# Merge gates take the place of retention's first head in the gaps of the projections, and the branch projections start inside the attention stage

## The chip, the cores and the metric

The kernel runs on one core of one Trainium2 chip, in one launch. The metric is device microseconds (us) of that core, the median of several runs; less is better. Engines are named as the profile names them: PE is TensorE (PEld its weight loads), DVE VectorE, ACT ScalarE, POOL GpSimd, SP the engine that issues most DMAs.

## The reference

One decoder block on x (1024 tokens by 1024 channels, float32). Only the parts around the change are spelt out.

```python
h = rms_norm(x, norm1_g)
z = h @ w_in                         # zq, zkv, zg (attention), zr (retention), zm (merge gates)
y_nsa = nsa_attention(zq, zkv, zg)   # compressed + selected + sliding-window branches, 8 heads of 64
y_ret = retention(q, k, v, g)        # zr: 4 parts (q, k, v, g) x 4 heads x 128 columns
u = einsum('nbsc,ncd->bsnd', stack([y_nsa, y_ret]), w_branch)     # two 512 -> 1024 projections
gates = sigmoid(zm)                  # 2 x 1024 columns of z
x = x + sum(gates * u) @ w_out
x = x + (silu(h2 @ w_gate) * (h2 @ w_up)) @ w_down                # h2 = rms_norm(x, norm2_g)
```

## The kernel before

**Order of the work.** The kernel writes a static program for each engine. A small planner inside the kernel decides the order while the program is built: every piece of work is a generator ("stream") that yields one instruction at a time; the planner keeps a modelled free time for each engine, and always emits the instruction that could start first by its model (ties on PE go to the lower priority number). On the chip each engine then runs its own list in order. So a stream with a high number fills PE wherever the streams of attention are, by the model, not ready; in this document such work is called fill.

**Matmuls.** All large products are float32 operands split in two parts (high and low), three matmuls of 128x128 by 128x512 for each block. A weight column tile of 128 columns over 1024 channels and 1024 tokens takes 2 halves x 8 x 3 = 48 matmuls (`half_mm`, 24 for each half). Where two such tiles are done together by the Winograd form of Strassen's scheme, the pair takes seven products of 12 matmuls, 84 in place of 96 (`g_main`, `g_prod`); its operand sums are made by DVE from the halves of H (`g_sums`), and of the weights (`g_wsums`, `g_fill`).

**Stages, in order of time.** (1) Norm, transposes and the token-major projections for q, k, v and the compressed branch (`a_mm`). In the gaps of the last of these, `ret_plain` runs the four projections of retention's head 0 plainly: k, v, q and g, 4 x 48 matmuls; what doesn't fit in the gaps follows them. (2) `g_main`: heads 1 to 3 of retention as six pairs of seven products each. (3) Attention (`cmp_all`, `produce_all`, `consume_all`), 16 units (2 groups x 8 query blocks), with retention's recurrence (`retention`) beside it, and as fill `merge_gates`: 16 column tiles, whose tanh ACT writes to tile zs and SP stores to z_scr. (4) When the last gate is done, the tile H (the normed input, no longer needed) is written over by the split outputs of the two branches (`y_loads`, `y_split`: tiles yraw to H); `branch1` multiplies retention's output with its half of w_branch, 16 half tiles of 12 matmuls in the two PSUM banks of f_ring, and `branch1_out` multiplies each by its gate (tile sg, loaded from z_scr) and stores it in u_scr. Stage 4 needs retention's pool to be closed (`late`). (5) `merge_main` waits for branch1 and for the last attention unit, and does the same 16 half tiles for the attention branch in the six banks of u_ring; `merge_out` loads gate and u_scr (tiles sgm and mx) and adds. (6) Output projection (`out_main`), norm, and the feed-forward part, which the change doesn't touch.

DMAs of these streams are all issued by SP, in the planner's order, but for the q tiles and group loads of attention, which POOL issues. DVE and ACT each run one list for all streams. `us` lists the attention units; `("y", us[-1])` is set when the last has been stored.

Of the kernel before, what the change touches and what calls it, by code (L numbers as in the profile page):

```python
# [9 lines left out]
F32 = mybir.dt.float32  # L10
F32R = mybir.dt.float32r
I32 = mybir.dt.int32
AF = mybir.ActivationFunctionType
# [3 lines left out]
T = 1024  # L17
# [241 lines left out]
def kernel(  # L259
# [199 lines left out]
    m_units = [[ntile(win, M0 + b * D + c * 128) for b in range(2)] for c in range(8)]  # L459
    rings = {"wo": None}  # L460
    o_units = [Unit(w_out[0][k * 128:(k + 1) * 128, :], lambda: rings["wo"]) for k in range(8)]
    r_plain = r_units[0]
    r_pairs = [(h, i) for h in range(1, 4) for i in (2, 0)]
    order = [u for c in range(7, -1, -1) for u in m_units[c][::-1]] + b_units[1] + b_units[0] + o_units

    def half_mm(hl, half, o, k0=0, nk=8, mov=None, step=1):
        n = 0
# [331 lines left out]

    def weights():  # L800
        yield Wait(lambda: "cmp" in fl)
        yield from split_units(r_plain)

    sch.spawn(load_units(r_plain), 5)
    sch.spawn(weights(), 3)
    sch.run(lambda: "cmp" in fl)
    cp.close()
# [21 lines left out]
    def unit(u):  # L829
        yield Wait(lambda: u.hl is not None)  # L830
# [9 lines left out]
        gm["S", j] = gpr.tile([128, 2, 4, 512], F32R, name=f"gS{j}")  # L840
    gt_ring = Bag([gpr.tile([128, 512], F32, name=f"gt{n}") for n in range(3)])

    def ret_plain():
        yield Wait(lambda: "rt" in fl)
        for i, u in enumerate(r_plain):
            yield from unit(u)
            for half in range(2):
                o = yield Alloc(f_ring)
                yield from half_mm(u.hl, half, o)
                t = yield Alloc(gt_ring)  # L850
                if i == 3:
                    yield ac(t, o, func=AF.Tanh, scale=0.5)
                    yield stt(t, t, 1.0, o, ALU.add, ALU.mult)
                else:
                    yield ac(t, o)
                f_ring.release(o)
                yield dma(r_scr[0][i][:, half * 512:half * 512 + 512], t)
                gt_ring.release(t)
            u.release()
        fl.add("plain")  # L860
# [55 lines left out]
    graw_ring = Slots([g_raw(n) for n in range(4)], lambda n: n % 4)  # L916

    def g_loads():
        yield Wait(lambda: all(u.raw is not None for u in r_plain))
        gm["raw"] = [(yield Alloc(raw_ring)), (yield Alloc(raw_ring))]  # L920
        for f, (h, i) in enumerate(r_pairs):
            if f:
                yield Wait(lambda: "gp" in fl)
            for n in range(2):
                t = yield Alloc(graw_ring)
                yield dma(t, r_units[h][i + n].src)
                gm["GU"[n], f] = t
        fl.add("gl")
        for i in range(2):
            yield Wait(lambda: i not in graw_ring.held)  # L930
            raw_ring.release(gm["raw"][i])
        yield from load_units(order)
# [7 lines left out]
    gop_ring = Slots([g_op(n) for n in range(8)], lambda n: n % 8 if n < 7 * GN - 6 else 4 + n % 4)  # L940

    def g_ops():
        yield Wait(lambda: all(u.hl is not None for u in r_plain))
        gm["h"] = [(yield Alloc(hl_ring))]
        made = set()
        for n, (p, f) in enumerate(gseq):
            yield Wait(lambda: ("G", f) in gm)
            G = gm["G", f]
            if n == 2:
                gm["h"].append((yield Alloc(hl_ring)))  # L950
            if n >= 4:
                yield Wait(lambda: "gp" in fl)
            if p in (1, 2):
                src, then = G[:, 4 * p - 4:4 * p], None
            else:
                yield Wait(lambda: ("U", f) in gm)
                U = gm["U", f]
                if p in (5, 6) and f not in made:
                    made.add(f)
                    sch.spawn(g_wsums(f, G, U), 2)  # L960
                if p == 5:
                    yield Wait(lambda: f in gT1)
                    src, then = gT1[f], lambda f=f: g_drop(f)
                elif p == 6:
                    yield Wait(lambda: f in gT2)
                    src, then = gT2[f], lambda f=f: fl.add(("g6", f))
                elif p == 7:
                    yield Wait(lambda: f in gT2)
                    src = yield Alloc(gm["Ta"])
                    yield tt(src, U[:, 4:8], U[:, 0:4], ALU.subtract)  # L970
                    then = lambda c=src: gm["Ta"].release(c)
                elif p == 4:
                    yield Wait(lambda: f in gT4)
                    src, then = gT4[f], lambda f=f: gm["Tb"].release(gT4[f])
                else:
                    src, then = U[:, 4:8], lambda U=U: graw_ring.release(U)
            o = yield Alloc(gop_ring)
            sch.spawn(g_fill(p, f, o, src, then), 2)
        for i in range(2):
            yield Wait(lambda: all(2 * i + j not in gop_ring.held for j in range(2)))  # L980
            hl_ring.release(gm["h"][i])
        yield from split_units(order)
# [215 lines left out]
        fl.add("ret")  # L1198

    sch.spawn(g_sums(), 7, 500.0)  # L1200
    sch.spawn(ret_plain(), 6)
    sch.spawn(g_loads(), 5)
    sch.spawn(g_ops(), 3)
    sch.spawn(g_main(), 8)
# [54 lines left out]
    zp_ring = ps_ring("S")  # L1259

    def merge_gates():
        for c in range(7, -1, -1):
            for b in (1, 0):
                um = m_units[c][b]
                yield from unit(um)
                z_scr[c, b] = dram.tile([128, T], F32, name=f"z_scr{c}_{b}")
                for half in range(2):
                    ring = f_ring if ("ret" in fl or "r0" not in fl) and f_ring.can() else zp_ring
                    o = yield Alloc(ring)
                    yield from half_mm(um.hl, half, o)  # L1270
                    sch.spawn(gate_out(c, b, half, o, ring), 4)
                um.release()
        fl.add("gates")
# [296 lines left out]
        fl.add(("u1", c, half))  # L1570

    def merge_main():
        yield Wait(lambda: "b1" in fl and ("y", us[-1]) in fl)
        for c, half in b0_order:
            yield from unit(b_units[0][c // 2])
            sch.spawn(merge_out(c, half), 1)
            yield from branch_mm(0, c, half, u_ring)
            if c % 2 and half:
                b_units[0][c // 2].release()
        fl.add("u_done")  # L1580

    b0_order = [(c, half) for c in range(4) for half in range(2)] + [(c, half) for half in range(2) for c in range(4, 8)]

    def mx_loads():
        for c, half in b0_order:
# [1 line left out]
            yield dma(mx[c // 2][:, c % 2, s], u_scr[c][:, s])  # L1587
            fl.add(("mx", c, half))

    def merge_out(c, half):  # L1590
        s = slice(half * 512, half * 512 + 512)
        yield Wait(lambda: ("mx", c, half) in fl)
        m = mx[c // 2][:, c % 2, s]
        sgm = yield Alloc(sg_ring)
        yield dma(sgm, z_scr[c, 0][:, s])
        yield Wait(lambda: (c, 0, half) in ups)
        yield stt(sgm, sgm, 1.0, ups[c, 0, half], ALU.add, ALU.mult)
        u_ring.release(ups[c, 0, half])
        yield tt(m, m, sgm, ALU.add)
        fl.add(("mix", c, half))  # L1600
        sg_ring.release(sgm)
# [6 lines left out]
    lts = ExitStack()  # L1608
    lt = lts.enter_context(tc.tile_pool(name="lt", bufs=1, side="right"))
    late["yraw"] = sb_ring(lt, [128, 512], F32, "yraw", 6)  # L1610
    late["sg"] = sb_ring(lt, [128, 512], F32, "sg", 4)
    fl.add("late")
    sch.run(lambda: ("y", us[-1]) in fl)
    sch.run(lambda: all(("yt", b, half, k) in fl for b in range(2) for half in range(2) for k in range(4))
# [699 lines left out]
```

## Time and profile before

| | us |
|---|---|
| median of 3 runs (lowest, highest) | 1615.13 (1609.12, 1615.92) |
| the profiled execution | 1612.77 |
| its span, first to last instruction | 1611.0 |
| PE busy in the span | 1564.9 (97%) |
| DVE busy | 1084.1 (67%) |
| ACT busy | 737.4 (46%) |
| mean granted PE clock | 0.992 of full |

Busy time is the union of an engine's instructions. The profile's rows give, for a group of instructions, how many there are, their busy time, the mean of one, and the idle time of the engine just before them with what ended it. A granted clock of 1.00 is 2.4 GHz, 0.5 is 1.2 GHz, and a stretch with a value between saw both.

### The profile page before, as it was taken

What the parts mean: (1) busy time and instruction counts of PE and PEld (TensorE: products, weight loads), DVE (VectorE), ACT (ScalarE), POOL (GpSimd) and SP (SyncE); (2) the same over time, 40 slices, a digit from 0 to 9 for tenths busy, and PEclk for the clock granted to TensorE, in tenths of its full rate; (3) what the DMA queues carried; (4) which work ended last, traced back from release to release, by engine and by line L of the source; (5) the groups of instructions that cost most, each with busy time, mean ns of one, the idle gap of its engine ahead of it and who ended that gap; (6) DMA issues with size and microseconds to landing.
All of it is one profiled execution on the core that took longest, in us unless ns stands there. A gap on an engine that the chain in (4) does not pass through costs nothing.

```text
span 1611.0 us, 23610 instructions
## 1 busy us (share of the span) xinstructions
PE 1564.9 (97%) x8332; PEld 1342.8 (83%) x8332; DVE 1084.1 (67%) x2624; ACT 737.4 (46%) x1498; POOL 243.2 (15%) x308
## 2 busy tenths in 40 slices
PE   7999999999999999999799999999999999999999
PEld 7998988879889888888588887888888888788887
DVE  7568775437889787885537668755666565477674
ACT  5233343347677676775312425433333333254442
POOL 2011000021321102310000000332334332000000
PEclk9999999999999999999999999999999999999999
DMA  6564363263332434121877323533344544397521
GB/s 189 145 191 132 112 196 122 91 199 96 103 107 84 144 119 126 59 66 46 254 241 268 119 91 92 183 131 131 131 144 131 180 139 140 125 397 265 178 78 53
DMA packets 191767, 233.62 MB, mean 145 GB/s; under 512 B 21920, under 2 KB 123296, under 8 KB 191392
## 3 DMA queue, kind: packets, MB, share of 16 engines
q1 hardware_dynamic: 179168, 194.36, 36.8%
q0 software_dynamic: 12480, 37.75, 7.0%
q8 instruction: 65, 1.06, 0.3%
q14 instruction: 54, 0.44, 0.1%
HBM read 159.70 MB, written 72.37 MB: 144 GB/s over the span
## 4 chain that ended last, share of the span: by engine, by line
PE 78%; DVE 10%; DMA 6%; ACT 3%; issue 2%; SPq 1%; POOL 1%; DVEq 0%; ACTq 0%; POOLq 0%
PE psS L314 26%; PE psF L314 25%; PE psO L314 12%; PE psT L314 11%; PE psT L319 4%; DVE P L1293 1%; DMA sg<-z_scr 1%; DMA cX<-c_scr 1%; DVE pT L344 1%; DVE nw L354 1%; SPq L368 1%; DMA yraw<-y_scr 1%; ACT P L334 1%; DMA mx<-u_scr 1%; DVE H L344 1%
## 5 line engine op out<-in xcount | busy, mean ns | idle before, releaser
L314 PE MATMUL psF<-H,wh 128*128 128x512 f32 x876 | 223.5, 399 | 11.3 <-DVE sg L354 9.3
L314 PEld LDWEIGHTS psF<-H,wh 128*128 128x128 f32 x876 | 163.9, 191 | 44.9 <-DVE sg L354 11.5
L314 PE MATMUL psS<-H,wh 128*128 128x512 f32 x732 | 199.9, 401 | 0.5 <-DVE sgm L354 0.5
L314 PEld LDWEIGHTS psS<-H,wh 128*128 128x128 f32 x732 | 133.9, 190 | 22.7 <-issue 0.9
L334 ACT ACTIVATE P<-P,pm 128x640 f32<-128x640 f32 (+7 forms) x128 | 94.0, 735 | 54.9 <-DVE pm L1293 53.6
L344 DVE TENSOR_TENSOR pT<-psT,pT 128x512 fp32r<-128x512 f32 (+1 forms) x152 | 91.6, 615 | 39.7 <-ACT pT L334 39.0
L314 PE MATMUL psS<-kT,qt 128*128 128x384 f32 (+3 forms) x384 | 103.2, 347 | 1.6 <-DMA kT<-k_scr 1.5
L334 ACT ACTIVATE pT<-psT 128x512 fp32r<-128x512 f32 (+1 forms) x152 | 77.3, 535 | 33.3 <-PE psT L319 32.8
L314 PE MATMUL psO<-pT,vv 128*128 128x256 f32 x528 | 89.6, 288 | 1.2 <-DVE pT L344 1.2
L314 PE MATMUL psS<-whA,H 128*128 128x256 f32 (+1 forms) x672 | 88.9, 289 | 0.0
L314 PEld LDWEIGHTS psO<-pT,vv 128*128 128x128 f32 x528 | 78.8, 189 | 9.5 <-DVE pT L344 2.3
L314 PEld LDWEIGHTS psS<-whA,H 128*128 128x128 f32 x672 | 84.7, 192 | 0.0
L319 PE MATMUL psT<-ident,P 128*128 128x128 f32 x528 | 76.7, 273 | 0.8 <-DVE pT L344 0.6
L334 ACT ACTIVATE wh<-wraw 128x512 fp32r<-128x512 f32 (+1 forms) x57 | 47.1, 836 | 60.7 <-PE psF L314 27.8
L314 PEld LDWEIGHTS psS<-kT,qt 128*128 128x128 f32 x384 | 65.7, 192 | 9.5 <-DMA kT<-k_scr 2.1
L344 DVE TENSOR_TENSOR wh<-wraw,wh 128x512 fp32r<-128x512 f32 (+1 forms) x56 | 54.6, 983 | 27.3 <-ACT wh L334 23.9
L319 PEld LDWEIGHTS psT<-ident,P 128*128 128x128 f32 x528 | 61.0, 140 | 4.9 <-issue 0.8
L334 ACT ACTIVATE op<-T 128x512 fp32r<-128x512 f32 x55 | 34.6, 630 | 63.3 <-PE psT L314 34.1
L314 PE MATMUL psS<-wo,H 128*128 128x512 f32 x216 | 58.5, 392 | 0.0
L344 DVE TENSOR_TENSOR op<-T,op 128x512 fp32r<-128x512 f32 x55 | 47.9, 876 | 15.4 <-ACT op L334 14.5
L314 PE MATMUL psS<-op 128*128 128x512 f32 x234 | 57.6, 389 | 0.0
L314 PE MATMUL psF<-sh,op 128*128 128x512 f32 x216 | 52.1, 390 | 2.0 <-DVE sh L344 2.0
(504 smaller groups left out, 3460.5 us busy)
## 6 DMA issues: line engine op xcount, KB each, us to landing
wraw<-in_w_in_dram SPq DMA_DIRECT2D x26, 512.0 KB, 3.9
row<-in_ffn_w_down_dram POOLq DMA_DIRECT2D x22, 512.0 KB, 5.6
f_scr<-fs SPq DMA_DIRECT2D x22, 512.0 KB, 2.8
t_scr<-row POOLq DMA_DIRECT2D x22, 512.0 KB, 3.2
qt<-q_scr POOLq DMA_DIRECT2D x16, 512.0 KB, 4.2
z_scr<-zs SPq DMA_DIRECT2D x32, 256.0 KB, 2.0
st<-t_scr SPq DMA_DIRECT2D x31, 256.0 KB, 4.8
wraw<-in_ffn_w_gate_dram SPq DMA_DIRECT2D x12, 512.0 KB, 3.5
```

The source lines that it names most:

```text
L314: lambda: pe.matmul(o, l, r, start=start, stop=stop, skip_group_check=True))
L319: return Op("pe", 109, 100, [o], [i], lambda: pe.transpose(o, i, ident))
L334: return Op("act", c, 150, outs, ins, lambda: act.activation(o, i, func, scale=scale, **kw))
L344: return vop(o, [a, b], lambda: (eng or dve).tensor_tensor(o, a, b, op), eng)
L354: return vop(o, ins, lambda: (eng or dve).scalar_tensor_tensor(o, a, s, b, op0=op0, op1=op1), eng)
L368: Op("sp", 50, 0, [o], [i], lambda: sp.dma_start(o, i))
L1293: lambda: dve.tensor_tensor_reduce(o, a, b, -sc, init, ALU.add, ALU.min, acc))
```

## The change

Retention's head 0 joins the seven-product scheme: `r_pairs` now starts at head 0, so that `g_main` has eight pairs and not six. Its place in the gaps of the token-major projections goes to four column tiles of the merge gates, (7,1), (7,0), (6,1), (6,0), in `gates_first`, which stores its tanh straight into z_scr; `merge_gates` starts at tile column 5. `merge_main` no longer waits for the last attention unit before its first product: its first two half tiles, both of the first 512 tokens, use f_ring, and only the third waits. `b0_order` is changed so that two tiles of the first half come before two of the second. The ring of sg tiles grows from 4 to 6. The diff:

```diff
--- before.py
+++ after.py
@@ -459,9 +459,10 @@
     m_units = [[ntile(win, M0 + b * D + c * 128) for b in range(2)] for c in range(8)]
     rings = {"wo": None}
     o_units = [Unit(w_out[0][k * 128:(k + 1) * 128, :], lambda: rings["wo"]) for k in range(8)]
-    r_plain = r_units[0]
-    r_pairs = [(h, i) for h in range(1, 4) for i in (2, 0)]
-    order = [u for c in range(7, -1, -1) for u in m_units[c][::-1]] + b_units[1] + b_units[0] + o_units
+    z_first = [(7, 1), (7, 0), (6, 1), (6, 0)]
+    z_units = [m_units[c][b] for c, b in z_first]
+    r_pairs = [(h, i) for h in range(4) for i in (2, 0)]
+    order = [u for c in range(5, -1, -1) for u in m_units[c][::-1]] + b_units[1] + b_units[0] + o_units
 
     def half_mm(hl, half, o, k0=0, nk=8, mov=None, step=1):
         n = 0
@@ -799,9 +800,9 @@
 
     def weights():
         yield Wait(lambda: "cmp" in fl)
-        yield from split_units(r_plain)
-
-    sch.spawn(load_units(r_plain), 5)
+        yield from split_units(z_units)
+
+    sch.spawn(load_units(z_units), 5)
     sch.spawn(weights(), 3)
     sch.run(lambda: "cmp" in fl)
     cp.close()
@@ -840,21 +841,17 @@
         gm["S", j] = gpr.tile([128, 2, 4, 512], F32R, name=f"gS{j}")
     gt_ring = Bag([gpr.tile([128, 512], F32, name=f"gt{n}") for n in range(3)])
 
-    def ret_plain():
-        yield Wait(lambda: "rt" in fl)
-        for i, u in enumerate(r_plain):
+    def gates_first():
+        for (c, b), u in zip(z_first, z_units):
             yield from unit(u)
+            z_scr[c, b] = dram.tile([128, T], F32, name=f"z_scr{c}_{b}")
             for half in range(2):
                 o = yield Alloc(f_ring)
                 yield from half_mm(u.hl, half, o)
                 t = yield Alloc(gt_ring)
-                if i == 3:
-                    yield ac(t, o, func=AF.Tanh, scale=0.5)
-                    yield stt(t, t, 1.0, o, ALU.add, ALU.mult)
-                else:
-                    yield ac(t, o)
+                yield ac(t, o, func=AF.Tanh, scale=0.5)
                 f_ring.release(o)
-                yield dma(r_scr[0][i][:, half * 512:half * 512 + 512], t)
+                yield dma(z_scr[c, b][:, half * 512:half * 512 + 512], t)
                 gt_ring.release(t)
             u.release()
         fl.add("plain")
@@ -916,7 +913,7 @@
     graw_ring = Slots([g_raw(n) for n in range(4)], lambda n: n % 4)
 
     def g_loads():
-        yield Wait(lambda: all(u.raw is not None for u in r_plain))
+        yield Wait(lambda: all(u.raw is not None for u in z_units))
         gm["raw"] = [(yield Alloc(raw_ring)), (yield Alloc(raw_ring))]
         for f, (h, i) in enumerate(r_pairs):
             if f:
@@ -940,7 +937,7 @@
     gop_ring = Slots([g_op(n) for n in range(8)], lambda n: n % 8 if n < 7 * GN - 6 else 4 + n % 4)
 
     def g_ops():
-        yield Wait(lambda: all(u.hl is not None for u in r_plain))
+        yield Wait(lambda: all(u.hl is not None for u in z_units))
         gm["h"] = [(yield Alloc(hl_ring))]
         made = set()
         for n, (p, f) in enumerate(gseq):
@@ -1198,7 +1195,7 @@
         fl.add("ret")
 
     sch.spawn(g_sums(), 7, 500.0)
-    sch.spawn(ret_plain(), 6)
+    sch.spawn(gates_first(), 6)
     sch.spawn(g_loads(), 5)
     sch.spawn(g_ops(), 3)
     sch.spawn(g_main(), 8)
@@ -1259,7 +1256,7 @@
     zp_ring = ps_ring("S")
 
     def merge_gates():
-        for c in range(7, -1, -1):
+        for c in range(5, -1, -1):
             for b in (1, 0):
                 um = m_units[c][b]
                 yield from unit(um)
@@ -1570,16 +1567,19 @@
         fl.add(("u1", c, half))
 
     def merge_main():
-        yield Wait(lambda: "b1" in fl and ("y", us[-1]) in fl)
-        for c, half in b0_order:
+        yield Wait(lambda: "b1" in fl)
+        for n, (c, half) in enumerate(b0_order):
             yield from unit(b_units[0][c // 2])
-            sch.spawn(merge_out(c, half), 1)
-            yield from branch_mm(0, c, half, u_ring)
+            ring = f_ring if n < 2 else u_ring
+            if n == 2:
+                yield Wait(lambda: ("y", us[-1]) in fl)
+            sch.spawn(merge_out(c, half, ring), 1)
+            yield from branch_mm(0, c, half, ring)
             if c % 2 and half:
                 b_units[0][c // 2].release()
         fl.add("u_done")
 
-    b0_order = [(c, half) for c in range(4) for half in range(2)] + [(c, half) for half in range(2) for c in range(4, 8)]
+    b0_order = [(c + d, half) for c in (0, 2) for half in range(2) for d in range(2)] + [(c, half) for half in range(2) for c in range(4, 8)]
 
     def mx_loads():
         for c, half in b0_order:
@@ -1587,7 +1587,7 @@
             yield dma(mx[c // 2][:, c % 2, s], u_scr[c][:, s])
             fl.add(("mx", c, half))
 
-    def merge_out(c, half):
+    def merge_out(c, half, ring):
         s = slice(half * 512, half * 512 + 512)
         yield Wait(lambda: ("mx", c, half) in fl)
         m = mx[c // 2][:, c % 2, s]
@@ -1595,7 +1595,7 @@
         yield dma(sgm, z_scr[c, 0][:, s])
         yield Wait(lambda: (c, 0, half) in ups)
         yield stt(sgm, sgm, 1.0, ups[c, 0, half], ALU.add, ALU.mult)
-        u_ring.release(ups[c, 0, half])
+        ring.release(ups[c, 0, half])
         yield tt(m, m, sgm, ALU.add)
         fl.add(("mix", c, half))
         sg_ring.release(sgm)
@@ -1608,7 +1608,7 @@
     lts = ExitStack()
     lt = lts.enter_context(tc.tile_pool(name="lt", bufs=1, side="right"))
     late["yraw"] = sb_ring(lt, [128, 512], F32, "yraw", 6)
-    late["sg"] = sb_ring(lt, [128, 512], F32, "sg", 4)
+    late["sg"] = sb_ring(lt, [128, 512], F32, "sg", 6)
     fl.add("late")
     sch.run(lambda: ("y", us[-1]) in fl)
     sch.run(lambda: all(("yt", b, half, k) in fl for b in range(2) for half in range(2) for k in range(4))
```

## Rows read from the trace of the kernel before

**Rows 1.** The page, part 1: busy time, share, instructions of two engines
```profile
PE 1564.9 (97%) x8332; PEld 1342.8 (83%) x8332; DVE 1084.1 (67%) x2624; ACT 737.4 (46%) x1498; POOL 243.2 (15%) x308
```

**Rows 2.** Busy time by stage: PE, PEld, DVE, ACT, POOL (instructions), clock, DMA share, GB/s
```profile
196.00:334.00 138.00, 137.31 (x607) 113.36 (x606) 78.15 (x119) 53.99 (x91) 0.00 (x0) 1.00 0.43 136
334.00:764.00 430.00, 421.34 (x2709) 376.49 (x2708) 332.28 (x1183) 297.77 (x723) 84.00 (x149) 0.99 0.33 103
764.00:876.00 112.00, 102.15 (x426) 82.21 (x425) 57.88 (x79) 24.09 (x33) 2.77 (x1) 0.95 0.80 262
```

**Rows 3.** Groups of instructions, 334 to 764: the gates' matmuls (fill) in two bank kinds
```profile
L314 PE MATMUL psS<-H,wh 128*128 128x512 f32 x408 | 123.1, 410 | 0.0
L314 PE MATMUL psF<-H,wh 128*128 128x512 f32 x317 | 87.4, 396 | 0.0
```

**Rows 4.** PE in order of time: start, us, instructions [idle before <- releaser]
```profile
763.77 15.13 PE L314 MATMUL psF<-H,wh 128*128 128x512 f32 x66
780.51 3.03 PE L314 MATMUL psF<-H,wh 128*128 128x512 f32 x12 [1.62 <-DVE sg L354]
787.59 8.29 PE L314 MATMUL psF<-H,wh 128*128 128x512 f32 x24 [4.05 <-DVE sg L354]
...
805.31 26.78 PE L314 MATMUL psF<-H,wh 128*128 128x512 f32 x108 [2.83 <-DVE sg L354]
831.92 8.32 PE L314 MATMUL psS<-H,wh 128*128 128x512 f32 x36
...
876.15 1.07 PE L314 MATMUL psS<-wo,H 128*128 128x512 f32 x4
```

**Rows 5.** Who waited for whom, 764 to 876: us in total, times, longest
```profile
DVE sgm L354 <- DMA sgm<-z_scr: 12.4, 4, 5.1
...
DVE yraw L344 <- DMA yraw<-y_scr: 10.1, 5, 4.6
...
PE psF L314 <- DVE sg L354: 9.3, 4, 4.1
```

**Rows 6.** A window with a lowered clock (columns as in group 2)
```profile
785.00:790.00 5.00, 2.41 (x6) 1.92 (x7) 3.14 (x5) 1.26 (x2) 0.00 (x0) 0.62 0.82 259
```

**Rows 7.** SP in order of time: the 24th of 32 gate stores, and the last y store
```profile
691.27 0.33 SPq L368 DMA_DIRECT2D z_scr<-zs  x1
...
764.59 0.37 SPq L368 DMA_DIRECT2D y_scr<-y  x1
```

**Rows 8.** The last 74 us of attention: window (columns as group 2), then groups
```profile
690.00:764.00 74.00, 74.00 (x458) 66.06 (x457) 52.16 (x136) 48.68 (x94) 6.72 (x11) 1.00 0.15 51
...
L314 PE MATMUL psF<-H,wh 128*128 128x512 f32 x150 | 41.2, 397 | 0.0
...
L344 DVE TENSOR_TENSOR pT<-psT,pT 128x512 fp32r<-128x512 f32 (+1 forms) x32 | 19.8, 636 | 11.1 <-ACT pT L334 11.1
```

**Rows 9.** DVE groups, 764 to 876: the work of stage 4
```profile
L354 DVE SCALAR_TENSOR_TENSOR sg<-sg,psF 128x512 f32<-128x512 f32 x16 | 11.0, 685 | 17.5 <-PE psF L314 12.0 <-DMA sg<-z_scr 5.5
L344 DVE TENSOR_TENSOR H<-yraw,H 128x512 fp32r<-128x512 f32 x16 | 10.6, 686 | 6.1 <-ACT H L334 6.0
...
L344 DVE TENSOR_TENSOR yraw<-yraw 128x512 f32<-128x512 f32 x8 | 5.5, 691 | 10.2 <-DMA yraw<-y_scr 10.1
```

**Rows 10.** DMA issues, KB, median us to landing: 690 to 764, then 764 to 876
```profile
y_scr<-y SPq DMA_DIRECT2D x2, 256.0 KB, 2.2
...
y_scr<-y SPq DMA_DIRECT2D x1, 256.0 KB, 4.3
```

**Rows 11.** Tile yraw: ns min/median/max of one issue; ACT's split; loads to landing
```profile
L368 SPq DMA_DIRECT2D yraw<-y_scr x40: 319/544/702, 606.7 to 798.3; - x40
L334 ACT ACTIVATE H<-yraw x16: 614/624/637, 768.6 to 804.7; 128x512 fp32r<-128x512 f32 x16
...
DMA to landing us min/median/max: 2.8/4.2/6.7
```

**Rows 12.** ACT groups, whole span: table loads
```profile
L334 ACT ACT_TABLE_LOAD x2 | 2.6, 1283 | 0.8 <-PEq L2300 0.8
```

## The prediction

> **What bounds the kernel now.** I read the page's first part, then busy time by stage, then the end of attention in PE's order of time with who waited for whom. PE is busy 97% of the span [rows 1], so the time is PE's work plus the few places where PE stands or runs slowly. By stage [rows 2] the seven-product stage is full (137.3 of 138 us), attention nearly so (421.3 of 430), and the stretch from 764 to 876 us loses most: 102.2 busy of 112, at a mean clock of 0.95. That stretch is what follows attention: the end of the gates, the retention branch (16 half tiles), the attention branch (16 half tiles), up to the first matmul of the output projection.
>
> Attention is full only because of its fill. 408 + 317 = 725 of the gates' 16 x 48 = 768 matmuls lie in it [rows 3]; 43 are left when the last product with v has ended, and then the 192 matmuls of branch1 run alone [rows 4], with nothing beside them that PE could do while it waits. The price of one 512-column matmul is 137.31 / 607 = 0.2262 us [rows 2]. From 763.77 to 876.15 [rows 4] are 112.4 us for 43 + 192 + 192 = 427 matmuls, or 96.6 us: 15.8 us are lost. 9.3 of them are waits for DVE's gated product, tile sg [rows 5]; most of the rest is slow matmuls after those waits, such as 24 in 8.29 us, which should be 5.4 [rows 4], in a stretch whose granted clock of 0.62 shows both levels, 1.2 and 2.4 GHz [rows 6].
>
> **The change, part by part.**
>
> *Work removed.* Head 0's four projections were 4 x 48 = 192 matmuls; two pairs of seven products are 2 x 84 = 168. The gates keep their number and only move. Net 24 x 0.2262 = **-5.4 us**. The seven-product stage grows by 168 x 0.2262 = 38.0 us; its DVE was busy 78 of 138 us [rows 2] and PE full, so the operand sums of two more pairs hide beside PE as those of six do. If that cover were gone, the stage would show PE idle, of which it now has 0.7 us.
>
> *The gaps of the projections.* Four gate tiles are 192 matmuls as before, by the same loads, splits, banks and stores; eight tanh replace six copies and two tanh on ACT, and DVE loses two products. Both functions come without a reload: there are two table loads in the whole span [rows 12]. I take nothing for it.
>
> *Where the fill goes.* Attention now has 576 gate matmuls, 192 of branch1 and 24 early ones of the attention branch: 792, against the 725 it used. So, if attention used as much as before, 67 matmuls (15.2 us) remain at its end, then 168. The 15.8 us lost now come from branch1 standing alone; inside attention its waits have other matmuls beside them. **-15.8 us**, from which three new costs are taken.
>
> *The changeover.* Gates end where the 24th of the 32 gate stores is now, 691 us [rows 7], plus the 38 us. Branch1 then waits for the splits of retention's output into H. In that time there is no fill, but attention's own work: in the last 74 us, 150 matmuls were fill [rows 8], 34 us, so attention itself holds 54% of PE. What waits now for 9.3 us would then show for 46% of that, 4.3; the DMAs are quieter there, 0.15 busy [rows 8] against 0.80 [rows 2], and six sg tiles let loads run ahead, so I take **+3 us**. Bounds: 0, if attention covers it; 10.1, DVE's waits for yraw [rows 5], if each of them stops attention's list on DVE and so PE. SP is passed as well: the yraw and sg loads, 0.54 us an issue [rows 11], now stand ahead of attention's y stores, which nobody waits for before the end.
>
> *The end of attention.* DVE was busy 52.2 of the last 74 us [rows 8]. Into it come 14 splits, 6 adds and some 12 gated products: 14 x 0.686 + 6 x 0.691 + 12 x 0.685 = 22.0 us [rows 9], against 21.8 idle. 11.1 of that idle time is 32 short handoffs ahead of pT [rows 8], 0.35 us each, too short for an operation of 0.69; so some 11 us don't fit, and part of that is taken up by attention's buffers: I let attention grow by 5 us, between 0 and 22. PE isn't idle then but eats fill: 10.2 us of the 15.2 remain. What the third half tile waits for is the last y: ACT's copy and the store's issue, 0.8 us after the last product with v [rows 4, 7], 2.2 to 4.3 to landing [rows 10], eight issues of 0.54 [rows 11], 2.8 to 4.2 for the last load [rows 11], then add, ACT's split and DVE's, 2.0 [rows 9, 11]: 12.2 to 15.7. I say 13.5, nearer the low end, since the DMAs are quiet there. So 3.3 us are not covered, and the slow matmuls behind a wait (8.29 - 5.4 = 2.9 us for one [rows 4]) add perhaps 1.7: **+5 us**. Bounds: 0 if attention doesn't grow; 22 - 15.2 + 13.5 + 2.9 = 23 if it grows by the whole 22.
>
> [...]
>
> *The attention branch after that.* Gates and u_scr for it load as now, and DVE waited 12.4 us for them [rows 5] with almost no idle PE, because six banks lay between. Two half tiles are now outstanding ahead of those six, so PE needs the first free bank up to two half tiles, 2 x 12 x 0.2262 = 5.4 us, earlier against the loads. Bounds 0 and 5.4; I take **+2 us**, since the loads also start sooner.
>
> **Sum**, against the profiled execution's own 1612.8 us (median of the runs 1615.1, so it is one of the quicker ones): -5.4 - 15.8 + 3 + 5 + 2 = -11.2, or **1602 us**.
>
> **The rivals.**
>
> *All of it is covered* (1594). Attention grows by 2 us or less and the changeover hides: new costs of 2 to 3 us, -19. For it: DVE's idle time equals the added work almost exactly. Against: the handoffs.
>
> *The loss only moves* (1610). Changeover 6, end 9, loads 3: 18 of the 21.2 are given back. For it: the yraw loads come in the same burst, right after the gates, and PE's list is fixed, so a wait that the planner didn't foresee now stops attention as well.
>
> *DVE becomes the bound, slower* (1625). Its place is DVE's list after the last gate. An add that waits for its load holds everything behind it; such waits now take 10.1 us, up to 4.6 at once [rows 5], and behind them would stand attention's own exponent sums and splits. With the 22 us added in full: -21.2 + 23 + 10.1 = +12, 1625. It decides from the point where attention's growth and these stops together pass 21 us. Against it: half of DVE's idle time is usable, and the adds for the first group's heads find their data long stored. The page "TensorE: Matmul & The Clock Gate" of the Trainium skill (Architectural detail) says that VectorE and ScalarE are strict first in, first out, while TensorE can pull weight loads ahead; by that rule nothing passes a waiting add, and the trace agrees so far that PE waited 9.3 us for DVE's gated products in the stretch in which DVE waited 10.1 us for yraw [rows 5].
>
> *The change doesn't do what it says*: if branch1 didn't start inside attention, because its inputs or the closing of retention's pool were late, only the 5.4 us would be left. The first yraw load, which needs that pool closed, is issued at 606.7 us [rows 11], long before the last gate, so I count this within the second rival.
>
> **How the numbers follow.** Forecast 1602, chance 0.46 (1598 to 1608); all covered 0.17; the loss only moves 0.30; DVE bound 0.07. About 0.5%, 8.1 us, is what a measurement of this kernel can tell from no change: faster means below 1607.1. The forecast's cases but for a few hundredths, and those of full cover, are below it: 0.62 faster, 0.31 the same, 0.07 slower. The range leaves out the slow rival and the low edge of the best case, and goes to the upper end of the second: 1592 to 1616.
>
> **What would show it.** Right: a seven-product stage some 38 us longer without idle PE; matmuls of branch1 among attention's; from the last product with v to the first of the output projection about 60 us, not 112. Wrong: PE idle after the last gate by more than 6 us, or over 8 us of it between the second and third half tile of the attention branch; attention longer than 440 us; or a new wait in the gaps of the projections, where I took nothing.

## The result, and the profile after

The changed kernel takes 1596.88 us (median of 4 runs, 1596.58 to 1599.25), against 1614.62 us of the kernel before on the same chip (median of 4, 1609.12 to 1615.92): a ratio of 0.990, 95% interval 0.9875 to 0.9925. The profiled execution took 1596.70 us, 16.1 less than the profiled one of before; the medians differ by 17.7. The forecast was 1602 us, range 1592 to 1616.

The page's first part, and then the busy time by stage (columns as in [rows 2]). The third line, from 727 us on, is the part of attention in which the splits of retention's output and branch1 now lie.

```profile
PE 1555.3 (98%) x8308; PEld 1335.0 (84%) x8308; DVE 1092.0 (68%) x2646; ACT 744.1 (47%) x1512; POOL 244.1 (15%) x308
```

```profile
196.00:372.00 176.00, 175.31 (x773) 144.82 (x773) 95.62 (x146) 67.34 (x115) 0.00 (x0) 1.00 0.42 130
372.00:809.50 437.50, 428.33 (x2731) 381.10 (x2730) 349.95 (x1214) 303.48 (x732) 87.39 (x150) 0.99 0.39 125
727.00:809.50 82.50, 81.05 (x485) 71.19 (x485) 71.06 (x173) 54.76 (x104) 10.03 (x12) 1.00 0.52 166
809.50:859.40 49.90, 48.79 (x215) 39.57 (x213) 30.41 (x43) 11.68 (x14) 0.00 (x0) 1.00 0.87 301
```

There are 24 matmuls fewer than in [rows 1]. The first line of the second fence answers to the seven-product stage, the last to the 112 us of [rows 2]: that stretch is now 49.9 us long, full, and at a granted clock of 1.00 where it was 0.95. DVE is busy for 71.1 of 82.5 us while branch1 lies in attention, against 52.2 of 74 [rows 8], and PE still stands for only 1.45 us there.

The fill in attention (groups of instructions, 372 to 809.5 us), and PE in order of time from the last product with v on:

```profile
L314 PE MATMUL psS<-H,wh 128*128 128x512 f32 x408 | 123.6, 411 | 0.0
L314 PE MATMUL psF<-H,wh 128*128 128x512 f32 x339 | 93.1, 396 | 0.0
```

```profile
809.03 0.64 PE L314 MATMUL psO<-pT,vv 128*128 128x256 f32 x4
809.50 10.14 PE L314 MATMUL psF<-H,wh 128*128 128x512 f32 x44
819.49 8.75 PE L314 MATMUL psS<-H,wh 128*128 128x512 f32 x36
828.07 2.88 PE L314 MATMUL psO<-H,wh 128*128 128x512 f32 x12
...
840.22 5.73 PE L314 MATMUL psS<-H,wh 128*128 128x512 f32 x24 [1.11 <-DVE sgm L354]
...
859.39 0.39 PE L314 MATMUL psS<-wo,H 128*128 128x512 f32 x1
860.44 1.89 PE L314 MATMUL psS<-wo,H 128*128 128x512 f32 x7 [0.66 <-DVE sgm L354]
```

747 fill matmuls lie in attention, against 725 [rows 3]. The 44 in psF that follow it are the last 20 of branch1 and the 24 of the two early half tiles. From 809.50 to 859.39 us are 49.9 us for 44 + 168 = 212 matmuls, or 48.0 us of work: 1.9 us are lost where [rows 4] lost 15.8. Not one wait for sg [rows 5] is left there.

How the last y reaches its product: SP's issues, then DVE's adds and splits (the last two channel tiles), each in order of time, then the DMA issues of this stretch (count, KB, median us to landing).

```profile
810.33 0.37 SPq L368 DMA_DIRECT2D y_scr<-y  x1
...
812.78 5.11 SPq L368 DMA_DIRECT2D yraw<-y_scr  x8
```

```profile
818.83 0.69 DVE L344 TENSOR_TENSOR H<-yraw,H 128x512 fp32r<-128x512 f32 x1 [0.70 <-ACT H L334]
820.13 0.69 DVE L344 TENSOR_TENSOR yraw<-yraw 128x512 f32<-128x512 f32 x1 [0.61 <-DMA yraw<-y_scr]
821.53 0.69 DVE L344 TENSOR_TENSOR H<-yraw,H 128x512 fp32r<-128x512 f32 x1 [0.70 <-ACT H L334]
```

```profile
yraw<-y_scr SPq DMA_DIRECT2D x8, 128.0 KB, 3.0
...
y_scr<-y SPq DMA_DIRECT2D x1, 256.0 KB, 2.4
```

The last split ends at 821.53 + 0.69 = 822.2 us, 12.7 us after the last product with v. Yet PE had gone on to the third half tile at 819.49 us, with no wait in the list; its line of 36 matmuls took 8.75 us where 36 took 8.32 before [rows 4].

**The ledger.** Work removed: 24 x 0.2262 = -5.4 us. The stretch behind attention loses 1.9 and not 15.8 us: -13.9. Attention lasts 438.0 us (371.55 to 809.50) and not 430.5, of which 22 more fill matmuls are 5.0: +2.5. The seven-product stage ends 38.24 us later, where 168 matmuls are 38.0: +0.2. A wait at the start of the output projection: +0.7. Together -15.9; the spans differ by 16.0. The ledger compares one profiled execution of each kernel; the executions of the kernel before alone spread over 6.8 us, so its terms of a microsecond or less belong to these two executions.

### The profile page after: what moved, and what is told of

Same layout as the page of the kernel before. It is cut to its first block, busy times and chain, and to the rows that moved or that the text cites. A ratio compares the mean times of both kernels' runs of the same rounds, so it can differ in the third digit from the quotient of the medians.

```text
span 1595.0 us, 23596 instructions
## 1 busy us (share of the span) xinstructions
PE 1555.3 (98%) x8308; PEld 1335.0 (84%) x8308; DVE 1092.0 (68%) x2646; ACT 744.1 (47%) x1512; POOL 244.1 (15%) x308
## 4 chain that ended last, share of the span: by engine, by line
PE 80%; DVE 11%; DMA 4%; ACT 3%; issue 2%; POOL 1%; SPq 1%; DVEq 0%; POOLq 0%; ACTq 0%
PE psS L314 28%; PE psF L314 24%; PE psO L314 12%; PE psT L314 12%; PE psT L319 4%; DVE P L1290 1%; DVE pT L344 1%; DMA cX<-c_scr 1%; DVE nw L354 1%; DMA yraw<-y_scr 1%; ACT P L334 1%; PE psF L319 1%; DVE H L344 1%; SPq L368 1%; DVE wh L344 1%
## 5 line engine op out<-in xcount | busy, mean ns | idle before, releaser
L314 PE MATMUL psS<-H,wh 128*128 128x512 f32 x756 | 206.6, 402 | 1.1 <-DVE sgm L354 1.1
L314 PE MATMUL psF<-H,wh 128*128 128x512 f32 x708 | 180.6, 394 | 1.9 <-ACT aw L334 1.9
L314 PEld LDWEIGHTS psS<-H,wh 128*128 128x128 f32 x756 | 138.5, 190 | 24.9 <-DVE sgm L354 1.5
L314 PEld LDWEIGHTS psF<-H,wh 128*128 128x128 f32 x708 | 129.8, 188 | 25.9 <-ACT aw L334 2.7
L334 ACT ACTIVATE P<-P,pm 128x640 f32<-128x640 f32 (+7 forms) x128 | 94.0, 735 | 53.5 <-DVE pm L1290 52.2
L344 DVE TENSOR_TENSOR wh<-wraw,wh 128x512 fp32r<-128x512 f32 (+1 forms) x53 | 49.9, 948 | 22.5 <-ACT wh L334 22.4
L344 POOL TENSOR_TENSOR T<-wraw 128x512 f32<-128x512 f32 x18 | 24.4, 1358 | 222.5 <-DMA wraw<-in_ffn_w_up_dram 219.9
```

The lines of the kernel that those rows point to most:

```text
L314: lambda: pe.matmul(o, l, r, start=start, stop=stop, skip_group_check=True))
L334: return Op("act", c, 150, outs, ins, lambda: act.activation(o, i, func, scale=scale, **kw))
L344: return vop(o, [a, b], lambda: (eng or dve).tensor_tensor(o, a, b, op), eng)
```

## The experiments

The theory after the result: nearly all of the gain is the 24 matmuls and the move of branch1 beside attention. The rival: part of it comes from the early start, the order, the banks or the two more sg tiles. Each run is compared with the kernel before on the same chip.

**e1: the moved work alone.** The changed kernel with the old `merge_main`, the old order, the old banks and four sg tiles.

```diff
-        yield Wait(lambda: "b1" in fl)
-        for n, (c, half) in enumerate(b0_order):
+        yield Wait(lambda: "b1" in fl and ("y", us[-1]) in fl)
+        for c, half in b0_order:
...
-            yield from branch_mm(0, c, half, ring)
+            yield from branch_mm(0, c, half, u_ring)
...
-    b0_order = [(c + d, half) for c in (0, 2) for half in range(2) for d in range(2)] + [(c, half) for half in range(2) for c in range(4, 8)]
+    b0_order = [(c, half) for c in range(4) for half in range(2)] + [(c, half) for half in range(2) for c in range(4, 8)]
...
-    late["sg"] = sb_ring(lt, [128, 512], F32, "sg", 6)
+    late["sg"] = sb_ring(lt, [128, 512], F32, "sg", 4)
```

> The changed kernel with only the moved work: head 0 in seven products and four gate tiles in the gaps, but the attention branch's loop, its order of half tiles, its banks and the four sg tiles as before. Theory (the gain is 24 matmuls plus branch1 beside attention; the new order only covers the last y's way through memory): branch1 still runs among attention's matmuls; after the last product with v some 20 matmuls of branch1 and 12 of the first half tile are left, 32 x 0.2262 = 7.2 us, against 12 us that the last y takes, so PE idles 4 to 5 us ahead of the second half tile and runs slowly after it for up to 2.9: 1601 to 1605 us. Rival (the early start and the new order are most of the gain): only the 24 matmuls come, 1609 us.

Measured: 1597.74 us (1597.63 to 1599.02), ratio 0.9899 (0.9883 to 0.9915). Both expectations were too high: the moved work alone gives the whole gain. PE in order of time shows why:

```profile
808.72 4.70 PE L314 MATMUL psF<-H,wh 128*128 128x512 f32 x20
813.26 4.24 PE L314 MATMUL psS<-H,wh 128*128 128x512 f32 x18
818.11 1.23 PE L314 MATMUL psS<-H,wh 128*128 128x512 f32 x3 [0.60 <-ACT H L334]
820.72 5.32 PE L314 MATMUL psS<-H,wh 128*128 128x512 f32 x15 [1.39 <-ACT H L334]
```

20 matmuls of branch1, then 18: the whole first half tile (tokens 0 to 511, 12 matmuls) and the first two channel tiles of the second (3 each). Then PE waits for ACT's split of the third channel tile and of the fourth, 2.0 us in all. A half tile doesn't wait for the last y as a whole, as the prediction had it: each group of three matmuls needs one channel tile, the last y feeds only the third and the fourth of them, and these arrive one after the other.

**e2: the rest alone.** The kernel before with the early start, the order, the banks and six sg tiles; head 0 and the gates stay where they were.

```diff
-        yield Wait(lambda: "b1" in fl and ("y", us[-1]) in fl)
-        for c, half in b0_order:
+        yield Wait(lambda: "b1" in fl)
+        for n, (c, half) in enumerate(b0_order):
...
+            ring = f_ring if n < 2 else u_ring
...
-    late["sg"] = sb_ring(lt, [128, 512], F32, "sg", 4)
+    late["sg"] = sb_ring(lt, [128, 512], F32, "sg", 6)
```

> The kernel before with only the rest: early first two half tiles in the other banks, the new order of half tiles, six sg tiles; head 0 plain in the gaps. Theory: branch1 still stands alone after the last gate and ends long after attention, so nothing starts earlier; PE's waits for the gated product stay near 9.3 us: 1611 to 1617 us. Rival (depth of sg or the early start were what cost the 15.8 us): 1600 to 1606 us.

Measured: 1615.94 us (1611.75 to 1619.92), ratio 1.0005 (0.9993 to 1.0016). PE's waits from 764 to 880 us (total, times, longest):

```profile
PE psF L314 <- DVE sg L354: 9.9, 5, 4.5
```

The theory held: the waits of [rows 5] stay, with six sg tiles as with four. So the place of branch1 counts, not its buffers.

**e3: the old order only**, in the changed kernel: the second half tile is then of tokens 512 to 1023.

```diff
-    b0_order = [(c + d, half) for c in (0, 2) for half in range(2) for d in range(2)] + [(c, half) for half in range(2) for c in range(4, 8)]
+    b0_order = [(c, half) for c in range(4) for half in range(2)] + [(c, half) for half in range(2) for c in range(4, 8)]
```

> The changed kernel with the old order of half tiles, a first and a second half by turns. Theory: the second half tile now needs the last y, 12 matmuls (2.7 us) earlier in PE's list; cover falls from 44 to 32 matmuls, 7.2 us, against 12: 4 to 5 us idle, then up to 2.9 of slow matmuls: 1601 to 1605 us. Rival (the order of half tiles is of no weight, since DMA or DVE bound the stretch anyway): 1596 to 1598 us.

Measured: 1598.34 us (1596.21 to 1600.71), ratio 0.9900 (0.9885 to 0.9916), close to the rival's 1596 to 1598 and well below the theory's 1601. PE in order of time:

```profile
807.47 8.78 PE L314 MATMUL psF<-H,wh 128*128 128x512 f32 x38
816.96 1.22 PE L314 MATMUL psF<-H,wh 128*128 128x512 f32 x3 [0.70 <-ACT H L334]
819.29 1.23 PE L314 MATMUL psF<-H,wh 128*128 128x512 f32 x3 [1.11 <-ACT H L334]
```

1.8 us of waits, three matmuls at a time, as in e1. The new order saves at most that, which no median here can tell from nothing.

**e4: no early start**, six banks of u_ring for all half tiles, the new order kept.

```diff
-        yield Wait(lambda: "b1" in fl)
+        yield Wait(lambda: "b1" in fl and ("y", us[-1]) in fl)
...
-            ring = f_ring if n < 2 else u_ring
-            if n == 2:
-                yield Wait(lambda: ("y", us[-1]) in fl)
...
-            yield from branch_mm(0, c, half, ring)
+            yield from branch_mm(0, c, half, u_ring)
```

> The changed kernel with the wait for the last attention unit ahead of the first half tile again and all half tiles in the six banks; the new order and six sg tiles stay. Theory: the first two half tiles stand at the same place of PE's list, since branch1 ends only after the last product with v; what changes is two banks fewer in flight, so that PE waits for a free bank where it waits 1.1 us now, up to 5.4 more: 1597 to 1600 us, near 1598. Rival (the early start itself brings time, by having 24 matmuls inside attention): 5.4 us more, 1602 us.

Measured: 1599.69 us (1597.94 to 1600.44), ratio 0.9907 (0.9893 to 0.9921), the theory's value, but not by its reason: PE waits 1.0 us for sgm here, no more than the 1.11 of the changed kernel. In PE's list the half tiles stand at the same place; the early start gives other banks and nothing else, since with the new order the first two don't need the last y in either kernel.

**e5: four sg tiles** in the changed kernel.

```diff
-    late["sg"] = sb_ring(lt, [128, 512], F32, "sg", 6)
+    late["sg"] = sb_ring(lt, [128, 512], F32, "sg", 4)
```

> The changed kernel with four sg tiles in place of six; every engine's list of instructions stays the same, only waits for a free tile can differ. Theory: among attention's matmuls a half tile of branch1 takes some 6 us, longer than load, product and store of its sg tile together hold it, so nothing waits: 1596 to 1599 us. Rival (the two tiles more are what took PE's 9.3 us of waits for sg away): 1602 to 1606 us.

Measured: 1598.95 us (1595.88 to 1601.72), ratio 0.9907 (0.9884 to 0.9930). The theory held: the order of every engine is the same as with six, PE waits for sg nowhere, and the interval overlaps that of the changed kernel. The two tiles more buy nothing that can be measured.

**e7: branch1 back behind attention**, everything else as changed. This takes the cover away from both sides: attention has no fill left in its last part.

```diff
-        yield Wait(lambda: "gates" in fl and "late" in fl)
+        yield Wait(lambda: "gates" in fl and "late" in fl and ("y", us[-1]) in fl)
```

> The changed kernel with branch1 held back until the last attention unit is stored. Theory (attention's last 78 us have gaps that branch1 fills): some 172 matmuls, 39 us, move behind attention, where branch1 is alone again; attention's end gets shorter by less than that, as it waits for ACT and DVE, and the waits and slow matmuls of a lone branch1 (15 us before, fewer here since its inputs are loaded long ahead) come back: 1615 to 1640 us. Rival (PE is the bound of attention too, so fill only stretches it): attention shrinks by the full 39 us and the time is 1597 to 1606.

Measured: 1634.46 us (1632.19 to 1637.81), ratio 1.0136 (1.0114 to 1.0157): slower than before. The last 82 us of attention (columns as in [rows 2]), then PE's waits from 727 to 860 us:

```profile
727.00:809.00 82.00, 61.82 (x365) 51.57 (x363) 62.59 (x163) 54.08 (x106) 11.20 (x13) 0.94 0.26 78
```

```profile
PE psO L314 <- DVE pT L344: 13.8, 18, 3.6
PE psF L314 <- DVE sg L354: 2.8, 3, 1.2
```

PE is busy for 61.8 of 82 us, against 81.1 of 82.5 with branch1 inside. The handoffs ahead of pT, which cost PE 1.2 us in the same part of the changed kernel, are 13.8 us of PE's time at its products with v alone here, and attention ends hardly earlier: its last product with v is at 803.88 us, not 809.03. So attention lasts nearly as long with some 170 matmuls of branch1 as without them: its waits have room for them. (In the kernel before, gates filled that room, and branch1 stood behind.) Behind attention 92.9 us pass for 384 matmuls (804.34 to 897.21 us), so 6.0 are lost there, against 1.9 in the changed kernel and 15.8 before. Branch1 is as alone as it was before, but 14 of the 16 splits into H already lie inside attention.

**e8: twelve gate tiles.** The kernel before leaves out the gates of columns 7 and 6 (192 matmuls) and uses those of 5 and 4 in their place. Head 0 stays plain, the order old, sg has four tiles.

```diff
-    order = [u for c in range(7, -1, -1) for u in m_units[c][::-1]] + b_units[1] + b_units[0] + o_units
+    order = [u for c in range(7, -1, -1) for u in m_units[c][::-1] if c < 6] + b_units[1] + b_units[0] + o_units
...
-        for c in range(7, -1, -1):
+        for c in range(5, -1, -1):
...
+                if c > 3:
+                    z_scr[c + 2, b] = z_scr[c, b]
```

> The kernel before without the gates of tile columns 7 and 6 (192 matmuls left out; those of 5 and 4 are used in their place), so that the gates end inside attention while retention stays as it was. Theory: besides 192 x 0.2262 = 43.4 us of work, the loss of branch1 alone goes, less what the changed kernel still pays, 10 to 12 us: 1614 - 43 - 11 = 1560 (1557 to 1563). Rival (most of the 17 us came from the seven products of head 0 and a better full stage, not from branch1's place): only the work, 1571 us.

Measured: 1561.19 us (1559.56 to 1566.53), ratio 0.9685 (0.9661 to 0.9710). The difference is 51.4 us, of which 192 x 0.2262 = 43.4 is the work left out; 8.0 us are gained beyond it, since branch1 has come beside attention. PE at attention's end:

```profile
772.21 0.64 PE L314 MATMUL psO<-pT,vv 128*128 128x256 f32 x4
772.69 4.70 PE L314 MATMUL psF<-H,wh 128*128 128x512 f32 x20
777.23 4.24 PE L314 MATMUL psS<-H,wh 128*128 128x512 f32 x18
...
825.28 4.92 PE L314 MATMUL psS<-wo,H 128*128 128x512 f32 x21
```

From 772.69 to 825.28 us, 52.6 us pass for 20 + 192 = 212 matmuls (48.0): 4.6 us are lost, not 15.8. That is 11.2 us won, from which a longer attention takes 4.8: 440.5 us for 748 matmuls of fill (332.20 to 772.69 us), against 430.5 for 725. The pattern of e1 appears in a kernel that has nothing of the change but less fill.

**e9: four gate tiles twice.** The changed kernel computes the tiles of columns 7 and 6 a second time, as fill in attention; 192 matmuls more, and branch1 goes back behind attention of itself.

```diff
+    m_units[6:] = [[ntile(win, M0 + b * D + c * 128) for b in range(2)] for c in (6, 7)]
-    order = [u for c in range(5, -1, -1) for u in m_units[c][::-1]] + b_units[1] + b_units[0] + o_units
+    order = [u for c in range(7, -1, -1) for u in m_units[c][::-1]] + b_units[1] + b_units[0] + o_units
...
-        for c in range(5, -1, -1):
+        for c in range(7, -1, -1):
```

> The changed kernel with the four gate tiles of the gaps computed a second time among the others, 192 matmuls more fill in attention, so that the gates end after attention as before and branch1 stands alone; the seven products of head 0 stay. Theory: 1597 + 43.4 for the work + 10 to 12 for the lone branch1 = 1651 (1648 to 1654). Rival (branch1's place is worth nothing): 1640 us.

Measured: 1653.88 us (1652.84 to 1657.0), ratio 1.0258 (1.0237 to 1.0278). That is 57.0 us over the changed kernel, 43.4 of work and 13.6 beyond it. PE's waits from 690 to 905 us:

```profile
PE psF L314 <- DVE sg L354: 9.1, 7, 3.3
```

They are the waits of [rows 5] again, 9.1 against 9.3 us. PE at the start and at the end of the stretch behind attention:

```profile
808.28 15.32 PE L314 MATMUL psF<-H,wh 128*128 128x512 f32 x66
...
919.39 0.39 PE L314 MATMUL psS<-wo,H 128*128 128x512 f32 x1
```

The 111.1 us hold 426 matmuls (42 of the gates, 192 and 192), 96.4 us of work: 14.7 are lost, 12.8 more than in the changed kernel and nearly all of the 13.6. All 16 splits into H fall into this stretch again (813 to 849 us).

The last three runs ask how many gate tiles should leave attention. **e10: six tiles in the gaps.**

```diff
-    z_first = [(7, 1), (7, 0), (6, 1), (6, 0)]
+    z_first = [(7, 1), (7, 0), (6, 1), (6, 0), (5, 1), (5, 0)]
...
-        for c in range(5, -1, -1):
+        for c in range(4, -1, -1):
```

> The changed kernel with six gate tiles ahead of the seven products in place of four, so 96 matmuls of fill fewer in attention. Theory (fill just about meets attention's demand: 792 for 748 used): 52 matmuls are lacking, 12 us of PE idle inside attention, and the last y's way through memory, 12 us, has nothing beside it: 1607 to 1621 us. Rival (attention is PE's, so less fill shortens it): 1595 to 1600 us.

Measured: 1618.12 us (1615.48 to 1618.98), ratio 1.0029 (1.0018 to 1.0039). PE in order of time at attention's end:

```profile
828.81 0.62 PE L314 MATMUL psO<-pT,vv 128*128 128x256 f32 x3 [0.16 <-DVE pT L344]
829.27 1.54 PE L314 MATMUL psS<-H,wh 128*128 128x512 f32 x6
838.52 1.65 PE L314 MATMUL psS<-H,wh 128*128 128x512 f32 x3 [7.72 <-ACT H L334]
842.17 8.03 PE L314 MATMUL psS<-H,wh 128*128 128x512 f32 x26 [2.00 <-ACT H L334]
...
880.30 0.39 PE L314 MATMUL psS<-wo,H 128*128 128x512 f32 x1
```

No fill is left when attention ends, and the way of the last y, 12.7 us in the changed kernel, now shows as 9.7 us of waits: from 829.27 to 880.30 us 168 matmuls (38.0 us) take 51.0, so 13.0 are lost, 11.1 more than in the changed kernel. Before that attention itself had run short: with 52 matmuls of fill fewer, 11.8 us of work, it takes 434.7 us (from 394.55) against 438.0, so it loses 8.5 us more. The two are 19.6 of the 21.2 us that e10 is slower, as the theory had it. So four tiles are bounded on this side by the demand for fill of attention and of the last y's way.

**e11: two tiles in the gaps.**

```diff
-    z_first = [(7, 1), (7, 0), (6, 1), (6, 0)]
+    z_first = [(7, 1), (7, 0)]
...
-        for c in range(5, -1, -1):
+        for c in range(6, -1, -1):
```

> The changed kernel with two gate tiles in the gaps in place of four, so 96 matmuls more fill in attention; the gates end some 35 us ahead of attention's end, and 105 of branch1's 192 matmuls stand alone after it. Theory A (what costs is the changeover, loads and splits, when nothing stands beside it; a lone branch1 whose inputs are in place runs full): the gaps now hold 96 matmuls, still more than fit, so 1596 to 1600 us. Theory B (branch1 loses wherever it is alone, by its loads of sg): 105/192 of 12 us come back, 1603 us or more.

Measured: 1625.22 us (1620.41 to 1627.77), ratio 1.0071 (1.0047 to 1.0095), 28.3 us over the changed kernel. Theory A fell. Theory B holds for attention's end: 75.65 us (811.22 to 886.87) for 297 matmuls (67.2), 8.5 lost, 6.6 more than in the changed kernel. But the larger loss lies where neither theory looked. PE in order of time, the changed kernel first, then e11:

```profile
188.93 29.48 PE L314 MATMUL psF<-H,wh 128*128 128x512 f32 x129
218.25 2.88 PE L314 MATMUL psS<-H,wh 128*128 128x512 f32 x12
...
229.13 5.60 PE L314 MATMUL psS<-gS,op 128*128 128x512 f32 x24
234.57 2.88 PE L314 MATMUL psF<-gS,op 128*128 128x512 f32 x12
```

```profile
191.38 8.21 PE L314 MATMUL psF<-H,wh 128*128 128x512 f32 x35
199.43 2.88 PE L314 MATMUL psS<-H,wh 128*128 128x512 f32 x12
...
220.05 5.74 PE L314 MATMUL psS<-gS,op 128*128 128x512 f32 x15 [7.54 <-ACT gS L334]
229.88 5.24 PE L314 MATMUL psF<-gS,op 128*128 128x512 f32 x12 [4.08 <-ACT gS L334]
```

And two windows of e11 (columns as in [rows 2]):

```profile
210.00:220.00 10.00, 2.51 (x12) 1.74 (x10) 9.24 (x15) 1.89 (x3) 0.00 (x0) 0.88 0.74 227
220.00:230.00 10.00, 5.87 (x16) 4.30 (x16) 5.41 (x9) 3.49 (x8) 0.00 (x0) 0.67 0.44 134
```

The seven products start 19 us earlier, and their third kind needs operand sums, gS, that DVE and ACT haven't made yet: DVE is busy for 9.24 of 10 us with PE at 2.51. Waits of 7.54 and 4.08 us and a lowered clock follow; from 196 to 246 us this run does 149 matmuls against 222, 73 x 0.2262 = 16.5 us. With the 6.6 that is 23.1 of 28.3; some 3.3 us lie ahead of 130 us and were not followed.

**e6: nothing in the gaps**, all 16 tiles in attention.

```diff
-    z_first = [(7, 1), (7, 0), (6, 1), (6, 0)]
+    z_first = []
...
-        for c in range(5, -1, -1):
+        for c in range(7, -1, -1):
```

> The changed kernel with nothing in the gaps of the projections: all 16 gate tiles are fill of attention, head 0 stays in seven products. The number of matmuls is that of the changed kernel. Theory: two losses add. The gaps stay empty, 60 to 75 matmuls that lay in them, 14 to 17 us; and the gates again end after attention, so branch1 stands alone, 10 to 13 us: 1597 + 27 = 1624 (1620 to 1628). Rival (the gaps are filled by other work of that stage anyway): 1607 to 1610 us.

Measured: 1642.51 us (1640.0 to 1645.56), ratio 1.0188 (1.0165 to 1.0212), 14 us over the top of what was expected. PE's waits from 120 to 260 us, then from 700 to 930 us:

```profile
PE psS L314 <- ACT gS L334: 15.6, 2, 8.5
PE psT L318 <- DVE kcat L344: 5.3, 2, 4.9
PE psF L314 <- ACT gS L334: 3.4, 1, 3.4
```

```profile
PE psF L314 <- DVE sg L354: 7.4, 5, 2.2
```

The second fence was expected, the first not: 19.0 us of waits for the same operand sums as in e11, and 5.3 for DVE in the projections. No version that does the whole work was faster than the changed kernel.

## Why the prediction was right, and where it wasn't

*What bounds it, and the -15.8 us of branch1.* Right in mechanism. e8 gets branch1 beside attention by leaving fill out and gains 8.0 us beyond the work; e9 adds fill and loses 13.6 beyond it, with the sg waits of before; e7 moves it back alone and loses 37.6 us against the changed kernel, since attention then stands uncovered as well. 13.9 of the 15.8 came. What the prediction didn't separate is why a lone branch1 loses so much. Where all 16 splits into H share the stretch with it, 15.8 (before) and 14.7 us (e9) are lost; where 14 of them lie ahead, inside attention, 6.0 (e7) and 8.5 (e11). So 6 to 10 us go with the splits falling into the same stretch, and standing alone costs the rest; no run moves the splits by themselves, so this share isn't shown as a cause.

*Work removed.* Right: 24 matmuls; the seven-product stage ends 38.24 us later, against 38.0, with PE full.

*The gaps, at nothing.* The number was right, but the reason given was too narrow. From 134 to 196 us PE is busy for 59.1 us as before (59.3). What made it free is that the four tiles bring exactly 192 matmuls, 129 of them after the projections (29.3 us), and that these cover the operand sums: with two tiles (e11) the sums show. The prediction counted the same matmuls, loads and splits, but not what else of the kernel the tail covers.

*The changeover, +3.* About right: attention grew by 2.5 us beyond its additional fill, the end of the attention included. 1.9 of them lie behind the 24th gate store, where PE stands for 1.45 us, 1.2 of these for DVE's pT. DVE's waits for yraw came to 0.8 us from 727 to 809.5 us, not 10.1 [rows 5].

*The end of attention, +5.* **This is the term that was mis-sized.** Its parts came near the prediction: from the 24th gate store to the last product with v 77.6 us against 72.5, so 5.1 us of growth for the 5; 44 matmuls or 10.0 us of fill left, for 10.2; 12.7 us for the way of the last y, for 13.5. That the first two fit so well is partly luck: only 3.2 of the 5.1 us went to fill (164 matmuls against 150), and 9 more fill matmuls lay ahead of that store (586 against 577). That DVE's fuller list made attention grow isn't shown. The step that failed is "what the third half tile waits for is the last y". Only six of its twelve matmuls read what the last y brings. The first three of these found their channel tile split (819.5 us), so only the last three waited: the 12.7 - 10.0 = 2.7 us that fill didn't cover were spent on its first nine (2.0 us), and its line came out 0.4 us longer. e1 and e3 show the same with waits of 2.0 and 1.8 us, which is why their expectations (1601 and more) were missed on the same side; e10 shows what the way costs with no fill. The slow matmuls behind a wait (1.7 us) didn't come: the granted clock is 1.00 from 809.5 to 859.4 us.

One sign was worked out wrongly: from the last product with v to the output projection the prediction's own terms give 10.2 + 38.0 + 5 + 2 = 55 us, not about 60. It was 49.9.

*The banks, +2.* Right: waits of 1.11 and 0.66 us for sgm.

So new costs were about 5 us (1.9 + 0.7 + 2.5) and not 10, and the time came out between the forecast and the rival in which all is covered (1594).

*The rivals.* That the loss only moves would have needed 18 us of new costs. DVE as the bound had its place right, DVE's list behind the last gate: it is fuller there (71.1 of 82.5 us) than in any stage of [rows 2]. But its trigger, an add that waits long for its load, didn't come: 0.8 us inside attention and 1.5 behind it. The page "TensorE: Matmul & The Clock Gate" of the Trainium skill (Architectural detail) says that VectorE and ScalarE are strictly first in, first out; no run here contradicts it, but behind so short a wait nothing is queued for long. That the change might not do what it says is excluded by the 20 matmuls that branch1 had left at attention's end.

## What to carry to other kernels

Independent work is worth most where another stage waits on handoffs: with branch1's 192 matmuls alone behind attention that stretch lost 15.8 us, with most of them beside attention 1.9, and attention without them was only 5 us shorter (e7). Look also at where the preparation of such work lies (here the splits into H): 6 to 10 us went with its falling into the uncovered stretch. Before moving such work, count the demand of both places, because here four tiles is the best of the counts tried, six starve attention and the last y's way (e10) and two uncover operand sums in the earlier stage (e11). And price a late operand by the part of an accumulating product that needs it, not by the product's start.

## What the runs showed that was not expected

A block of matmuls between two stages covered another engine's preparation, which no wait in the trace of before names: shortened from 129 to 35 matmuls (29.5 to 8.2 us), it cost 16.5 us, more than the waits of 11.6 us, because the granted clock fell to 0.88 and 0.67 beside them: 15 matmuls in 5.74 us and 12 in 5.24, where 12 take 2.88 at full speed. And attention without fill is far from free of PE's waits: 13.8 us for pT in e7, with a granted clock of 0.94, where [rows 8] shows 11.1 us of the same handoffs on DVE and a full PE.
